# A hybrid RWKV-7 and attention layer: woven products placed at five dense stretches, and five head sums' roots spread to rows through DRAM

## The chip, the cores and the metric

The kernel runs on one core of a Trainium2 chip. The metric is the device time of one execution in microseconds, lower is better. A core has TensorE (PE), VectorE (DVE), ScalarE (ACT), GpSimd (POOL) and SyncE (SP), each with an instruction queue of its own. They meet through semaphores; DMAs are issued from a queue and run beside the engines.

## The reference

One layer computes, for 512 latent tokens on a grid and 128 context tokens of width 1024, an RWKV-7 branch (8 heads of 64, forward and backward), a neighbourhood attention branch, merges and a feed-forward block. Two formulas matter here: the norm of the keys of each head, and the norm of the recurrence's output of each head.

```python
kk = _heads(k * k_k)
kk = kk * lax.rsqrt(jnp.sum(kk * kk, axis=-1, keepdims=True) + L2_EPS)
...
def _wkv_step(s, inp):
    r, w, k, v, a, b = inp
    sa = jnp.einsum("bhvk,bhk->bhv", s, a)
    s = s * w[:, :, None, :] + sa[..., None] * b[:, :, None, :] + v[..., None] * k[:, :, None, :]
    return s, jnp.einsum("bhvk,bhk->bhv", s, r)
...
y = y_f + y_b
mean = jnp.mean(y, axis=-1, keepdims=True)
var = jnp.mean(jnp.square(y - mean), axis=-1, keepdims=True)
y = (y - mean) * lax.rsqrt(var + GN_EPS) * _heads(ln_g) + _heads(ln_b)
out = (y + bonus).reshape(bsz, t_len, RW_WIDTH) * gate
```

## The kernel before

After modulation, norm, the input products and the attention (0 to about 250 us) comes the recurrence (about 250 to 640 us), then the merges and the feed-forward block. Tiles hold channels on the 128 partitions and the 640 tokens along the row; a tile of 128 channels is two heads. The recurrence therefore runs over four groups, `ct` = 0 to 3, of two heads each. The tokens are cut into ten blocks of 64, for two directions: 20 lines.

A group has three parts, each a Python generator:

- `main` (two steps): `n_job` (L1191), small products that make the triangular matrices `Nt`.
- `inv`: inverts them. VectorE makes a chain of 30 steps `s` = 1 to 30 on the tile `RL` (L1297, then the pairs L1328 and L1332, or L1321), and transposes the result at L1345 and L1347, which TensorE reads at L1358. Beside the chain, at the steps in `jobs` (2, 9 and 28; in group 3: 2, 8 and 28), stand jobs of TensorE: `v_job` (L1248), `t_job` (64 products of 64x64, L1270) and `g_job` (128 more, L1212, L1215, L1248, L1259). Their masks (L1229, L1232) are VectorE's.
- `carry`: the state's chain over the blocks (TensorE L1399 to L1461, ScalarE L1422 and L1454, VectorE L1473), with `prep` of the next group beside it.

`out(ct - 1)`, the end of the group before (norm of each head, bonus, gate), and `bonus(ct)` (L1159 on TensorE, L1161 on VectorE) are advanced inside `inv(ct)`. `out(3)` comes behind the last carry.

The order on each engine is the order in which the program is written. The generator `weave` sets it: at every `yield` it takes the next entry of `PRM["plan"]`, three numbers: so many woven products, then so many steps of `out`, then of `bonus`. A woven product is a 128x128 by 128x320 product of another stage (L225, L589), of which there is a supply in every group; it depends on nothing in the recurrence. The weights of these products come as a high and a low half; the low half is made by an accumulating DMA from GpSimd's queue (L193).

Two places take a head's sum to all rows. In `prep_a` (L666 to L686) five products sum the squares of the keys into a tile `r` of [128 tokens x 10] (5 token blocks x 2 heads), GpSimd takes the power -1/2 (L671), ScalarE copies each value 64 times along the row (L676), TensorE transposes the five blocks (L681), and VectorE multiplies the keys by the result from PSUM (L684, L686) into `kk`. `out` does the same with `inv_sqrt_bcast` (L1130 sums, L1134, L1136 power, L1139 copy, L1144 transposes), and multiplies at L1497 and L1498. The steps of `out` stand between steps of the inverse's chain in VectorE's order.

Of the kernel before, what the change touches and what calls it, by code (L numbers as in the profile page):

```python
# [14 lines left out]
P = 128  # L15
# [12 lines left out]
    order=("l0 l1 k0 r0 v0 l2 g0 g1 g2 k1 g3 r1 g4 g5 v1 g6 g7 k2 r2 g8 g9 v2 g10 g11 k3 r3 g12 g13 v3 g15 g14 a0 a1 a2 "  # L28
     "a3 b0 b1 b2 b3"),
    plan=(  # L30
        "22.0 0.0 2.0 4.0",
        ("0.0.0 2.0.0 2.0.1 10.0.0 2.0.1 2.0.1 2.0.1 2.0.1 2.0.1 2.0.0 10.0.0 2.0.0 2.0.0 10.0.0 2.0.0 "
         "2.0.0 2.0.0 10.0.0 2.0.0 2.0.0 2.0.0 2.0.0 2.0.0 2.0.0 2.0.0 2.0.0 2.0.0 2.0.0 2.0.0 2.0.0 "
         "5.0.0 24.0.0 20.0.0 10.0.0 8.0.0 8.0.0 0.0.0"),
        ("10.0 1.0 7.1 5.2 0.0 7.1 7.2 0.0 7.1 7.2 0.0 8.1 12.2 0.0 7.1 7.2 0.0 7.1 7.2 0.0 6.1 6.2 "
         "0.0 8.1 7.2 6.0"),
        "22.0 2.0 2.0 2.0",
        ("0.0.0 0.0.0 2.0.1 10.0.0 1.0.0 2.1.1 2.1.1 2.1.1 2.1.1 1.1.1 10.0.0 3.1.0 2.0.0 2.0.0 2.0.0 "
         "2.1.0 2.1.0 10.0.0 2.1.0 2.1.0 2.1.0 2.1.0 2.1.0 2.1.0 12.0.0 2.0.0 2.0.0 2.0.0 2.0.0 2.0.0 "
         "5.0.0 24.0.0 20.0.0 10.0.0 8.0.0 8.0.0 0.0.0"),  # L40
        ("10.0 0.0 7.1 7.2 0.0 7.1 7.2 0.0 7.1 7.2 0.0 7.1 7.2 0.0 7.1 7.2 0.0 6.1 7.2 0.0 7.1 7.2 0.0 "
         "7.1 7.2 6.0"),
        "22.0 2.0 0.0 5.0",
        ("0.0.0 10.0.0 2.0.1 10.0.0 2.0.0 2.1.1 2.1.1 2.1.2 2.1.1 2.1.0 10.0.0 2.0.0 2.0.0 2.0.0 2.1.0 "
         "2.1.0 2.1.0 10.0.0 2.1.0 2.1.0 2.1.0 3.1.0 4.1.0 2.1.0 2.0.0 2.0.0 2.0.0 4.0.0 2.0.0 2.0.0 "
         "5.0.0 24.0.0 18.0.0 8.0.0 9.0.0 8.0.0 0.0.0"),
        ("10.0 0.0 8.1 14.2 0.0 7.1 7.2 0.0 7.1 7.2 0.0 0.1 6.2 0.0 7.1 7.2 0.0 7.1 7.2 0.0 7.1 7.2 "
         "0.0 7.1 7.2 6.0"),
        "32.2 0.0 0.0 0.0",
        ("0.0.0 16.1.0 8.1.1 9.0.0 2.1.0 8.1.1 1.1.1 0.1.1 0.1.1 0.1.1 4.1.0 14.1.0 6.1.0 6.1.0 6.1.0 "  # L50
         "6.1.0 6.1.0 7.1.0 6.0.0 6.0.0 6.0.0 6.0.0 6.0.0 6.0.0 7.0.0 6.0.0 6.0.0 6.0.0 6.0.0 6.0.0 "
         "6.0.0 6.0.0 11.0.0 8.0.0 8.0.0 2.0.0 0.0.0"),
        ("10.3 0.0 5.1 5.2 0.0 5.1 5.2 0.0 5.1 5.2 0.0 5.1 5.2 0.0 5.1 5.2 0.0 5.1 5.2 0.0 5.1 5.2 0.0 "
# [63 lines left out]
def body(ctx: ExitStack, tc: tile.TileContext, xs, xp, cols, consts, w_ada, b_row, w_rw, w_qkv,  # L117
# [380 lines left out]
    def pre_t():  # L498
        return kp.tile([P, 643], F32, tag="pre", bufs=4, name=nm("pre"))[:, :NT]
# [131 lines left out]
    def parts(ct, k):  # L631

        return ((0, 320), (320, NT)) if ct and PRM[k] else ((0, NT),)

    def prep_a(ct, S, tpps, mid=None):

        S.Dt = kp.tile([P, 2, 10], F32, tag="Dt", bufs=2, name=nm("Dt"))
        S.P65 = [None, None]
        S.pre = []
        S.BK = []  # L640

        def lora(d, tw, ta):
# [25 lines left out]
        yield 0, 0  # L668
        rk = kp.tile([P, 10], F32, tag="r10", bufs=2, name=nm("r10"))
        dve.tensor_scalar(out=rk, in0=ps[:, :10], scalar1=1.0, scalar2=1e-12, op0=ALU.mult, op1=ALU.add)  # L670
        pool.tensor_tensor(out=rk, in0=rk, in1=mhalf[:, :10], op=ALU.pow)  # L671
        S.pre.append((pre_t(), pre_t()))
        yield 0, 0.2
        yield from lora(0, *S.pre[0])
        for (a, b) in parts(ct, "pa"):
            act.copy(V(sqt, [[64, (b - a) // 64], [1, 64]], a), V(rk[:, :], [[1, (b - a) // 64], [0, 64]], a // 64))  # L676
        yield 2, 0
        pa, pb = tpps(), tpps()
        for i in range(5):
            o_ = pa[:, i * 128:(i + 1) * 128] if i < 4 else pb[:, :128]  # L680
            pe.transpose(o_, sqt[:, i * 128:(i + 1) * 128], ident)  # L681
        yield 0, 0
        S.kk = kk = kk_t()
        dve.scalar_tensor_tensor(out=kk[:, :512], in0=kt_[:, :512], scalar=col("kk", ct),  # L684
                                 in1=pa[:, :512], op0=ALU.mult, op1=ALU.mult)
        dve.scalar_tensor_tensor(out=kk[:, 512:], in0=kt_[:, 512:], scalar=col("kk", ct),  # L686
                                 in1=pb[:, :128], op0=ALU.mult, op1=ALU.mult)
        yield 0, 1.2
# [24 lines left out]

# [385 lines left out]
    with ExitStack() as s3:  # L1099
# [23 lines left out]
        def wps():  # L1123
            return pp.tile([P, 512], F32, tag="w", bufs=6, name=nm("w"))

        def inv_sqrt_bcast(sqt, scale, eps, ps_):

            ps = ps_()
            for i in range(5):
                pe.matmul(ps[:, 2 * i:2 * i + 2], sqt[:, i * 128:(i + 1) * 128], kc("blk2", 2),  # L1130
                          start=True, stop=True)
            yield
            r = kp.tile([P, 10], F32, tag="r10", bufs=2, name=nm("r10"))
            dve.tensor_scalar(out=r, in0=ps[:, :10], scalar1=scale, scalar2=eps, op0=ALU.mult,  # L1134
                              op1=ALU.add)
            pool.tensor_tensor(out=r, in0=r, in1=mhalf[:, :10], op=ALU.pow)  # L1136
            yield
            yield
            act.copy(c64(sqt), V(r[:, :], [[1, 10], [0, 64]]))  # L1139
            yield  # L1140
            pa, pb = ps_(), ps_()
            for i in range(5):
                o = pa[:, i * 128:(i + 1) * 128] if i < 4 else pb[:, :128]
                pe.transpose(o, sqt[:, i * 128:(i + 1) * 128], ident)  # L1144
            yield
            return pa, pb
# [146 lines left out]
        def inv(ct, S, late):  # L1293
# [11 lines left out]
            for s in range(1, 31):  # L1305
# [178 lines left out]
        def out(ct, S):  # L1484
# [4 lines left out]
            for hf in range(2):  # L1489
# [7 lines left out]
            dve.tensor_tensor(out=yc[:, :512], in0=yc[:, :512], in1=pa[:, :512], op=ALU.mult)  # L1497
            dve.tensor_tensor(out=yc[:, 512:], in0=yc[:, 512:], in1=pb[:, :128], op=ALU.mult)  # L1498
# [901 lines left out]
```

## Time and profile before

| | before |
|---|---|
| median of the runs (lowest to highest), us | 1136.23 (1135.29 to 1136.40) |
| the profiled execution, us | 1135.23 |
| its span, us | 1133.1 |
| mean granted TensorE clock | 0.997 |
| TensorE busy in the span | 97% |
| VectorE, ScalarE, GpSimd busy | 72%, 50%, 22% |

The span runs from the first to the last instruction in the trace; 2.1 us of the execution lie around it. A row of a timeline gives start and length in us, engine, line, operation, output and input tiles, shape and count; a bracket at its end is the idle time of the engine ahead of it and what ended it. "issue" there means that the trace shows nothing that the engine waited for.

### The profile page before, as it was taken

To read this page: it belongs to the slowest core of one execution; us is meant where nothing else is said; L and a number is where in the kernel's file an instruction comes from. 1 tells how busy PE (TensorE), PEld (TensorE's weight loads), DVE (VectorE), ACT (ScalarE), POOL (GpSimd) and SP (SyncE) were. 2 spreads that over 40 slices of the span, in tenths; PEclk is the share of its full clock that TensorE was granted. 3 is DMA by queue.
4 is the path that set the end of the run, shared out by engine and by line. 5 is a ranking of instruction groups with operands and counts; after the bars stand their busy time and mean duration, and the time that the engine had idled before them with its cause. 6 is when DMAs were issued, how large, how long until landed. Compare 5 with 4: busy or idle time off the path is not lost. (4 is left out here: it accounts for less than half of the span.)

```text
span 1133.1 us, 27124 instructions
## 1 busy us (share of the span) xinstructions
PE 1098.5 (97%) x11118; PEld 971.1 (86%) x11118; DVE 814.1 (72%) x1709; ACT 571.8 (50%) x1106; POOL 245.7 (22%) x318
## 2 busy tenths in 40 slices
PE   6999999999999999999899999999999999999998
PEld 4688878789888988888898788998999989989987
DVE  4565465669648937946787846899788887889854
ACT  4444566665566575467443534564453543444430
POOL 1163234321101111210100431151212122131100
PEclk9999999999999999999999999999999999999999
DMA  9753677644423453353743873477567567665622
GB/s 340 270 105 103 186 263 264 209 140 120 123 60 93 109 140 88 95 134 78 262 129 107 256 226 121 139 179 185 139 176 181 145 157 178 173 169 143 157 85 93
DMA packets 72995, 179.05 MB, mean 158 GB/s; under 512 B 8708, under 2 KB 23684, under 8 KB 72872
## 3 DMA queue, kind: packets, MB, share of 16 engines
q1 hardware_dynamic: 58488, 140.86, 37.8%
q0 software_dynamic: 12368, 33.56, 16.2%
q10 hardware_dynamic: 2016, 2.90, 0.8%
q8 instruction: 87, 1.43, 0.5%
q14 instruction: 36, 0.29, 0.1%
HBM read 137.81 MB, written 16.94 MB: 137 GB/s over the span
## 5 line engine op out<-in xcount | busy, mean ns | idle before, releaser
L1929 PE MATMUL f<-t,whi 128*128 128x320 f32 x640 | 141.8, 309 | 0.8 <-ACT whi L1974 0.5
L1929 PE MATMUL f<-b,whi 128*128 128x320 f32 x608 | 135.1, 310 | 0.4 <-DVE b L214 0.4
L225 PE MATMUL fl<-h,whi 128*128 128x320 f32 x672 | 121.1, 320 | 0.1
L1929 PEld LDWEIGHTS f<-t,whi 128*128 128x128 f32 x640 | 106.8, 188 | 1.4 <-ACT whi L1974 0.7
L225 PEld LDWEIGHTS fl<-h,whi 128*128 128x128 f32 x672 | 101.4, 188 | 4.9 <-issue 0.2
L1929 PEld LDWEIGHTS f<-b,whi 128*128 128x128 f32 x608 | 101.8, 188 | 1.2 <-issue 0.6
L1929 PE MATMUL f<-t,wlo 128*128 128x320 f32 x320 | 99.0, 309 | 0.2 <-DVE wlo L1977 0.2
L1929 PE MATMUL f<-b,wlo 128*128 128x320 f32 x304 | 94.0, 309 | 0.1
L194 ACT CAST whi<-wst 128x1024 fp32r<-128x1024 f32 (+1 forms) x67 | 69.0, 1031 | 38.6 <-PE acc L313 27.3
L313 PE MATMUL acc<-whi,h 128*128 128x512 f32 x240 | 78.5, 401 | 0.6 <-DVE h L438 0.6
L1974 ACT CAST whi<-ws 128x1024 fp32r<-128x1024 f32 x40 | 42.1, 1052 | 68.9 <-PE f L1929 42.2
L193 POOL DMA_DIRECT2D wlo<-wst x28 | 24.9, 888 | 192.6 <-ACT wlo L192 176.4
L197 DVE TENSOR_TENSOR wlo<-wst,whi 128x1024 fp32r<-128x1024 f32 (+2 forms) x47 | 48.1, 1033 | 25.7 <-ACT whi L194 25.5
L225 PE MATMUL fl<-h,wlo 128*128 128x320 f32 x336 | 62.7, 317 | 0.0
L1929 PEld LDWEIGHTS f<-t,wlo 128*128 128x128 f32 x320 | 60.1, 188 | 0.5 <-DVE wlo L1977 0.5
L1473 DVE TENSOR_TENSOR ZV<-w,Dt 64x128 f32<-64x128 f32 x64 | 18.4, 288 | 54.5 <-PE w L1461 53.3
L1929 PEld LDWEIGHTS f<-b,wlo 128*128 128x128 f32 x304 | 57.1, 188 | 0.4 <-DVE wlo L1977 0.4
L1988 POOL TENSOR_TENSOR ws<-wst 128x512 f32<-128x512 f32 x20 | 30.8, 1542 | 121.0 <-DVE wlo L1977 81.5
L1977 DVE TENSOR_TENSOR wlo<-ws,whi 128x1024 fp32r<-128x1024 f32 x40 | 53.7, 1342 | 4.1 <-ACT whi L1974 4.1
L313 PEld LDWEIGHTS acc<-whi,h 128*128 128x128 f32 x240 | 44.8, 188 | 12.5 <-issue 2.2
L225 PEld LDWEIGHTS fl<-h,wlo 128*128 128x128 f32 x336 | 51.2, 188 | 1.9
L984 POOL TENSOR_TENSOR L<-L,m 128x384 f32<-128x384 f32 (+1 forms) x40 | 32.1, 824 | 94.0 <-DVE m L983 75.1
(379 smaller groups left out, 2826.4 us busy)
## 6 DMA issues: line engine op xcount, KB each, us to landing
wst<-in_w_dram SPq DMA_DIRECT2D x58, 512.0 KB
wst<-in_w_rw_dram SPq DMA_DIRECT2D x31, 512.0 KB
wlo<-wst POOLq DMA_DIRECT2D x28, 512.0 KB, 4.8
wa<-in_w_ada_dram SPq DMA_DIRECT2D x24, 512.0 KB
f<-in_w_ada_dram SPq DMA_DIRECT2D x16, 512.0 KB
t<-in_w_dram SPq DMA_DIRECT2D x16, 512.0 KB
wst<-in_w_qkv_dram SPq DMA_DIRECT2D x12, 512.0 KB
o<-o_d SPq DMA_DIRECT2D x14, 320.0 KB
```

The lines of the kernel that those rows point to most:

```text
L193: pool.dma_start(lo[:, :n].bitcast(F32), st[:, :n], accum_op=ALU.add)
L194: act.copy(hi[:, :n], st[:, :n])
L197: dve.tensor_tensor(out=lo[:, a:b], in0=st[:, a:b], in1=hi[:, a:b].bitcast(F32), op=ALU.subtract)
L225: pe.matmul(ps[:, :t1 - t0], w[:, a:a + 128], x[:, k0 + kt, t0:t1], start=n == 0, stop=n == 3 * nk - 1)
L313: pe.matmul(pss[i][:, a:b], lhs(x, kt, ts_), w[:, cs_], start=ki == 0 and n == 0, stop=ki == last and n == 2)
L984: pool.tensor_tensor(out=L, in0=L, in1=V(m[:, :], [[0, w]], 3), op=ALU.mult)
L1473: dve.tensor_tensor(out=V(ZV[own, l + 1, h, :], [[128 * dl, 2], [1, 64]]), in0=V(pn[own, :], [[64, 2], [1, 64]], 64 * g), in1=V(Dt[own, 0, ...
L1929: pe.matmul(ps[:, :H2], w_[:, c_], x_[:, kt, :], start=first and kt + n == 0, stop=last and kt == 3 and n == 2, skip_group_check=more)
L1974: act.copy(r[0][:, :width], src())
L1977: dve.tensor_tensor(out=r[1][:, :width], in0=src(), in1=r[0][:, :width].bitcast(F32), op=ALU.subtract)
L1988: eng_x(PRM["se"][i - 1]).tensor_tensor(out=o_, in0=x, in1=y, op=op)
```

## The change

It has two parts.

The numbers of `plan` move woven products; within each group their sum stays. In group 0, six go from behind the first job of `inv` (step 2) to between the two jobs of `main`. In group 1, six go from behind that job to the start of `inv`, ahead of it. In groups 2 and 3 a new tuple `cut` names steps at which `inv` yields between `t_job` and `g_job`, so that an entry of the plan falls there: ten products at step 9 of group 2; two at step 28 of group 2, with six more ahead of `t_job`; six at step 8 of group 3, with three and four more at the two entries ahead. These came later in their groups before.

A new function `spread` takes the place of the copy, the transposes and the read from PSUM, in `prep` of groups 1, 2 and 3 (`if ct`) and in `out` of groups 0 and 1 (`far`). It writes `r` turned to DRAM, [10 x 128], and reads it back, each value to 64 rows, with one DMA for each head. All three DMAs stand on GpSimd's queue. VectorE then multiplies once, from SBUF. In `prep` the product moves behind the first direction's `exp` of `tw`; in `out` the number of yields stays.

```diff
     plan=(
-        "22.0 0.0 2.0 4.0",
-        ("0.0.0 2.0.0 2.0.1 10.0.0 2.0.1 2.0.1 2.0.1 2.0.1 2.0.1 2.0.0 10.0.0 2.0.0 2.0.0 10.0.0 2.0.0 "
+        "22.0 6.0 2.0 4.0",
+        ("0.0.0 2.0.0 2.0.1 4.0.0 2.0.1 2.0.1 2.0.1 2.0.1 2.0.1 2.0.0 10.0.0 2.0.0 2.0.0 10.0.0 2.0.0 "
...
-    wl="dddddddddppppppppppppppppppppppdddpdddd", nu=9, lg=14, jo=(2, 0, 1), na=(
+    wl="dddddddddppppppppppppppppppppppdddpdddd", nu=9, lg=14, jo=(2, 0, 1), cut=((), (), (9, 28), (8,)), na=(
...
+    def spread(r, t):
+
+        r_d = dp.tile([10, P], F32, name=nm("r_d"))
+        pool.dma_start(r_d.rearrange("c p -> p c"), r)
+        for h in range(2):
+            x = r_d[h]
+            pool.dma_start(V(t[hrows[h], :], [[128, 5], [1, 128]]),
+                           bass.AP(x.tensor, x.offset, [[0, 64], [256, 5], [1, 128]]))
...
         pool.tensor_tensor(out=rk, in0=rk, in1=mhalf[:, :10], op=ALU.pow)
+        if ct:
+            spread(rk, sqt)
...
+            if ct and not d:
+                dve.scalar_tensor_tensor(out=kk, in0=kt_, scalar=col("kk", ct), in1=sqt, op0=ALU.mult, op1=ALU.mult)
+                yield 0, 0.8
...
             pool.tensor_tensor(out=r, in0=r, in1=mhalf[:, :10], op=ALU.pow)
+            if far:
+                spread(r, sqt)
+                for _ in range(4):
+                    yield
+                return None, None
...
                     for f in (v_job, t_job):
                         f(S, *jobs[s])
+                    if s in PRM["cut"][ct]:
+                        yield
                     masks.append(g_job(S, *jobs[s]))
...
-            pa, pb = yield from inv_sqrt_bcast(ysq, 1.0 / 64, 64e-5, wps)
-            dve.tensor_tensor(out=yc[:, :512], in0=yc[:, :512], in1=pa[:, :512], op=ALU.mult)
-            dve.tensor_tensor(out=yc[:, 512:], in0=yc[:, 512:], in1=pb[:, :128], op=ALU.mult)
+            pa, pb = yield from inv_sqrt_bcast(ysq, 1.0 / 64, 64e-5, wps, ct < 2)
+            if ct < 2:
+                dve.tensor_tensor(out=yc, in0=yc, in1=ysq, op=ALU.mult)
+            else:
...
```

How it moves instructions. First TensorE in `inv` of group 2, at step 9, where `t_job` ends and `g_job` begins. Before:

```order
L1270 MATMUL w_6206<-K,f_833_5751 64x64
L1270 MATMUL w_6207<-K,f_833_5751 64x64
L1248 MATMUL w_6242<-K,vp_627 64x64 x2
L1212 MATMUL w_6243<-AG,f_833_5751 64x64 x2
L1215 MATMUL w_6244<-R__2901,f_833_5751 64x64
```

And now, with L1290 for L1270, L1268 for L1248 and L1232 for L1212; `fl` is the output of the woven products:

```order
L1290 MATMUL w_6194<-K,f_830_5734 64x64
L225 MATMUL fl_6122<-h_95,whi_5855 128x320
L225 MATMUL fl_6122<-h_92,whi_5855 128x320
L225 MATMUL fl_6122<-h_96,whi_5855 128x320
L225 MATMUL fl_6122<-h_92,whi_5855 128x320
L225 MATMUL fl_6122<-h_96,whi_5855 128x320
L225 MATMUL fl_6122<-h_89,wlo_5856 128x320 x2
L225 MATMUL fl_6122<-h_90,wlo_5856 128x320 x2
L225 MATMUL fl_6122<-h_91,wlo_5856 128x320
L1268 MATMUL w_6239<-K,vp_627 64x64 x2
L1232 MATMUL w_6240<-AG,f_830_5734 64x64 x2
```

Ten woven products that stood behind the whole job now stand between its two halves.

Second GpSimd's queue in `inv` of group 1, behind the power for `out(0)`. `U` is a tile of ScalarE's, `wlo` the low half of the next weights. Before:

```order
L1136 TENSOR_TENSOR r_725_4666<-r_725_4666,mhalf 128x10
L538 MEMSET U_4794 128x2
L539 MEMSET U_4794 128x1
L193 DMA wlo_4825<-wst_4602 128x1024
L214 TENSOR_TENSOR out_4627<-out_4627,yo_4898 128x320 x2
```

And now:

```order
L1151 TENSOR_TENSOR r_724_4660<-r_724_4660,mhalf 128x10
L638 DMA r_d_4663<-r_724_4660 128x10x1
L641 DMA pre_4622<-r_d_4663 64x5x128 x2
L538 MEMSET U_4792 128x2
L539 MEMSET U_4792 128x1
L193 DMA wlo_4822<-wst_4532 128x1024
L214 TENSOR_TENSOR out_4621<-out_4621,yo_4887 128x320 x2
```

Three DMAs stand ahead of the memsets and the next weight's DMA; the reads (L641) wait for the write's landing.

Third TensorE in the carry of group 0, where `prep(1)` transposed. Before:

```order
L225 MATMUL fl_3951<-h_92,whi_3719 128x320
L225 MATMUL fl_3951<-h_96,whi_3719 128x320
L681 MATMUL w_3986<-K,pre_3856 128x128 x4
L681 MATMUL w_3987<-K,pre_3856 128x128
L1419 MATMUL w_3998<-ZV,AG 64x64 x4
L1399 MATMUL w_3807<-TG,ZV 64x64 x4
```

And now (L1441 for L1419, L1421 for L1399):

```order
L225 MATMUL fl_3955<-h_92,whi_3719 128x320
L225 MATMUL fl_3955<-h_96,whi_3719 128x320
L1441 MATMUL w_3991<-ZV,AG 64x64 x4
L1421 MATMUL w_3807<-TG,ZV 64x64 x4
L1421 MATMUL w_3808<-TG,ZV 64x64 x4
```

The five transposes are gone, and the carry's products follow the same woven products directly.

More of the change, by code (lines that the diff above doesn't have):

```diff
@@ L37 @@
         "22.0 2.0 2.0 2.0",
-        ("0.0.0 0.0.0 2.0.1 10.0.0 1.0.0 2.1.1 2.1.1 2.1.1 2.1.1 1.1.1 10.0.0 3.1.0 2.0.0 2.0.0 2.0.0 "
+        ("6.0.0 0.0.0 2.0.1 4.0.0 1.0.0 2.1.1 2.1.1 2.1.1 2.1.1 1.1.1 10.0.0 3.1.0 2.0.0 2.0.0 2.0.0 "
          "2.1.0 2.1.0 10.0.0 2.1.0 2.1.0 2.1.0 2.1.0 2.1.0 2.1.0 12.0.0 2.0.0 2.0.0 2.0.0 2.0.0 2.0.0 "
@@ L43 @@
         "22.0 2.0 0.0 5.0",
-        ("0.0.0 10.0.0 2.0.1 10.0.0 2.0.0 2.1.1 2.1.1 2.1.2 2.1.1 2.1.0 10.0.0 2.0.0 2.0.0 2.0.0 2.1.0 "
-         "2.1.0 2.1.0 10.0.0 2.1.0 2.1.0 2.1.0 3.1.0 4.1.0 2.1.0 2.0.0 2.0.0 2.0.0 4.0.0 2.0.0 2.0.0 "
-         "5.0.0 24.0.0 18.0.0 8.0.0 9.0.0 8.0.0 0.0.0"),
+        ("0.0.0 10.0.0 2.0.1 10.0.0 2.0.0 2.1.1 2.1.1 2.1.2 2.1.1 2.1.0 10.0.0 0.0.0 2.0.0 2.0.0 2.0.0 2.1.0 "
+         "2.1.0 2.1.0 10.0.0 2.1.0 2.1.0 2.1.0 3.1.0 4.1.0 2.1.0 2.0.0 2.0.0 2.0.0 4.0.0 8.0.0 2.0.0 2.0.0 "
+         "5.0.0 16.0.0 18.0.0 8.0.0 9.0.0 8.0.0 0.0.0"),
         ("10.0 0.0 8.1 14.2 0.0 7.1 7.2 0.0 7.1 7.2 0.0 0.1 6.2 0.0 7.1 7.2 0.0 7.1 7.2 0.0 7.1 7.2 "
@@ L49 @@
         "32.2 0.0 0.0 0.0",
-        ("0.0.0 16.1.0 8.1.1 9.0.0 2.1.0 8.1.1 1.1.1 0.1.1 0.1.1 0.1.1 4.1.0 14.1.0 6.1.0 6.1.0 6.1.0 "
+        ("0.0.0 16.1.0 8.1.1 9.0.0 2.1.0 8.1.1 1.1.1 3.1.1 4.1.1 6.0.0 0.1.1 1.1.0 4.1.0 6.1.0 6.1.0 6.1.0 "
          "6.1.0 6.1.0 7.1.0 6.0.0 6.0.0 6.0.0 6.0.0 6.0.0 6.0.0 7.0.0 6.0.0 6.0.0 6.0.0 6.0.0 6.0.0 "
@@ L674, in prep_a @@
         yield from lora(0, *S.pre[0])
[L675 to L682, printed above, removed]
-        S.kk = kk = kk_t()
[L684 to L688, printed above, removed]
+        S.kk = kk = kk_t()
+        if ct:
+            yield 2, 0
+        else:
+            act.copy(c64(sqt), V(rk[:, :], [[1, 10], [0, 64]]))
+            yield 2, 0
+            pa, pb = tpps(), tpps()
+            for i in range(5):
+                o_ = pa[:, i * 128:(i + 1) * 128] if i < 4 else pb[:, :128]
+                pe.transpose(o_, sqt[:, i * 128:(i + 1) * 128], ident)
+            yield 0, 0
+            for (a, b, p_) in ((0, 512, pa), (512, NT, pb)):
+                dve.scalar_tensor_tensor(out=kk[:, a:b], in0=kt_[:, a:b], scalar=col("kk", ct),
+                                         in1=p_[:, :b - a], op0=ALU.mult, op1=ALU.mult)
+            yield 0, 1.2
         for d in range(2):
@@ L1124, in wps, with inv_sqrt_bcast @@
             return pp.tile([P, 512], F32, tag="w", bufs=6, name=nm("w"))
-        def inv_sqrt_bcast(sqt, scale, eps, ps_):
+        def inv_sqrt_bcast(sqt, scale, eps, ps_, far):
             ps = ps_()
@@ L1495, in out @@
                 yield
-            pa, pb = yield from inv_sqrt_bcast(ysq, 1.0 / 64, 64e-5, wps)
-            dve.tensor_tensor(out=yc[:, :512], in0=yc[:, :512], in1=pa[:, :512], op=ALU.mult)
-            dve.tensor_tensor(out=yc[:, 512:], in0=yc[:, 512:], in1=pb[:, :128], op=ALU.mult)
+            pa, pb = yield from inv_sqrt_bcast(ysq, 1.0 / 64, 64e-5, wps, ct < 2)
+            if ct < 2:
+                dve.tensor_tensor(out=yc, in0=yc, in1=ysq, op=ALU.mult)
+            else:
+                dve.tensor_tensor(out=yc[:, :512], in0=yc[:, :512], in1=pa[:, :512], op=ALU.mult)
+                dve.tensor_tensor(out=yc[:, 512:], in0=yc[:, 512:], in1=pb[:, :128], op=ALU.mult)
             act.activation(yc, yc, AF.Identity, scale=col("lg", ct), bias=col("lb", ct))
```

## The prediction

> **What bounds the kernel now.** I read the page's busy shares first, then the waits of TensorE in the recurrence (250 to 640 us), then the timelines of the places that the change touches. The first fence is the page's busy us, share and instructions of each engine; the second the waits: engine, its instruction, what it waited for, us in total, times, longest.
>
> ```profile
> PE 1098.5 (97%) x11118; PEld 971.1 (86%) x11118; DVE 814.1 (72%) x1709; ACT 571.8 (50%) x1106; POOL 245.7 (22%) x318
> ```
>
> ```profile
> PE w L1212 <- issue: 2.5, 2, 1.4
> PE w L1448 <- ACT x L1422: 2.1, 6, 0.6
> ...
> PE w L1215 <- DVE bv L1161: 1.6, 1, 1.6
> PE w L1215 <- issue: 1.2, 1, 1.2
> PE w L1191 <- issue: 1.0, 1, 1.0
> ...
> PE w L1270 <- issue: 0.9, 1, 0.9
> PE w L1358 <- DVE f L1345: 0.8, 2, 0.4
> ```
>
> TensorE is busy 97% of the span, so time comes out only where TensorE issues less or waits less. Five of these rows hold six single waits of 0.9 to 1.6 us in runs of small products (L1191, L1270, L1212, L1215). "issue" means that nothing in the program released it; I take it for TensorE running ahead of the loading of its own instructions, since these waits lie inside the runs of 64 to 192 small products that a job writes. That cause is inferred. The last row says that VectorE is a second bound: TensorE has twice waited for the inverse's chain on VectorE (L1345, read by L1358).
>
> The end of that chain in groups 1, 2 and 3 (VectorE), and TensorE's first read of it:
>
> ```profile
> 383.83 2.06 DVE L1345 STREAM_TRANSPOSE f<-RL 128x1024 f32<-128x1024 f32 x1
> ...
> 386.04 0.66 PE L1358 MATMUL w<-f,Nt 32*32 32x32 f32 x29 [0.36 <-DVE f L1345]
> ...
> 477.65 2.07 DVE L1345 STREAM_TRANSPOSE f<-RL 128x1024 f32<-128x1024 f32 x1
> ...
> 480.71 0.51 PE L1358 MATMUL w<-f,Nt 32*32 32x32 f32 x18
> ...
> 579.08 2.05 DVE L1345 STREAM_TRANSPOSE f<-RL 128x1024 f32<-128x1024 f32 x1
> ...
> 584.53 0.69 PE L1358 MATMUL w<-f,Nt 32*32 32x32 f32 x29
> ```
>
> In group 1 TensorE starts 0.15 us after the chain (383.83 + 2.06 = 385.89): VectorE sets the end. In group 2 the chain ends at 479.72, and 0.15 later TensorE could start, but it starts at 480.71: VectorE has 0.84 us to spare. In group 3 it has 584.53 - 581.13 - 0.15 = 3.25. So what TensorE saves inside the inverse counts in full in group 3, up to about 0.9 us in group 2, and not at all in group 1 (nor in group 0, the other of the two waits), unless the chain itself gets shorter.
>
> **The change part by part.** *Five transposes less, in five places.* What such a visit costs, from TensorE's timeline in group 1 (start, length of the row, line, count):
>
> ```profile
> 365.90 0.90 PE L225 MATMUL fl<-h,whi 128*128 128x320 f32 x5
> 366.63 0.71 PE L1144 MATMUL w<-K,pre 128*128 128x128 f32 x5
> 367.10 0.83 PE L225 MATMUL fl<-h,whi 128*128 128x320 f32 x4
> 367.76 1.33 PE L225 MATMUL fl<-h,wlo 128*128 128x320 f32 x8
> 368.93 0.75 PE L225 MATMUL fl<-h,whi 128*128 128x320 f32 x4
> ```
>
> Five woven products leave in 0.73 us and eight in 1.17, 0.147 each. From the five transposes to the fifth product behind them pass 1.13 us, of which four products are 0.59: a visit costs 0.54 us. Three lie in the preparations inside the carries of groups 0, 1 and 2, where TensorE goes straight on:
>
> ```profile
> 311.87 1.29 PE L225 MATMUL fl<-h,whi 128*128 128x320 f32 x7
> 313.00 0.71 PE L681 MATMUL w<-K,pre 128*128 128x128 f32 x5
> 313.63 0.45 PE L1419 MATMUL w<-ZV,AG 128*64 128x64 f32 x8
> ```
>
> Three times 0.54 is 1.6 us. The carry is a chain through ScalarE and VectorE too (the 2.1 us at L1448 above), so a part can turn into waiting: I take -1.4, ends -0.8 and -1.6. The later kk product is covered: the first reader of kk is L725 at 328.03, behind 2.13 us in which VectorE is idle, against a pow that ends near 307.5.
>
> ```profile
> 305.56 1.98 POOL L671 TENSOR_TENSOR r<-r,mhalf 128x10 f32<-128x10 f32 x1 [1.92 <-DVE r L670]
> ...
> 327.39 0.61 DVE L1473 TENSOR_TENSOR ZV<-w,Dt 64x128 f32<-64x128 f32 x2 [2.13 <-PE w L1461]
> 328.03 0.83 DVE L725 SCALAR_TENSOR_TENSOR NK<-pre,kk 128x640 f32<-128x640 f32 x1
> ```
>
> The other two visits are in out of groups 0 and 1, inside the inverses of groups 1 and 2, where by the above they are worth nothing by themselves (group 1) or at most what VectorE allows (group 2).
>
> *The trip through DRAM.* In out, VectorE's product (L1497) keeps its place in VectorE's order and now waits for the last of three DMAs that GpSimd issues behind the pow. VectorE is in order: behind the product stand the next steps of the inverse's chain, so each us that the trip is late is a us of the chain. The time that it has:
>
> ```profile
> 359.52 0.17 DVE L1134 TENSOR_SCALAR r<-w 128x10 f32<-128x10 f32 x1 [0.22 <-PE w L1130]
> 360.17 0.49 DVE L1161 TENSOR_TENSOR bv<-w,vp 128x320 f32<-128x320 f32 x1 [0.48 <-PE w L1159]
> ...
> 369.07 0.68 DVE L1497 TENSOR_TENSOR out<-out,w 128x512 f32<-128x512 f32 x1
> 369.67 0.28 DVE L1498 TENSOR_TENSOR out<-out,w 128x128 f32<-128x128 f32 x1
> ...
> 359.77 1.98 POOL L1136 TENSOR_TENSOR r<-r,mhalf 128x10 f32<-128x10 f32 x1 [5.99 <-DVE r L1134]
> ...
> 454.39 2.08 POOL L1136 TENSOR_TENSOR r<-r,mhalf 128x10 f32<-128x10 f32 x1 [7.58 <-DVE r L1134]
> ...
> 462.89 0.67 DVE L1497 TENSOR_TENSOR out<-out,w 128x512 f32<-128x512 f32 x1
> ```
>
> Group 1: 369.07 - 361.75 = 7.3 us, or 6.8 if the 0.48 us wait goes (below). Group 2: 462.89 - 456.47 = 6.4 us.
>
> The trip L is not in the trace. Its parts have neighbours: GpSimd's DMAs of 128 rows, and one of 256 pieces (128x2x512).
>
> ```profile
> 866.57 1.22 POOL L2077 DMA_DIRECT2D t<-in_w_dram  x1
> ...
> L193 POOL DMA_DIRECT2D wlo<-wst x28 | 24.9, 888 | 192.6 <-ACT wlo L192 176.4
> ...
> wlo<-wst POOLq DMA_DIRECT2D x28, 512.0 KB, 4.8
> ...
> q0 software_dynamic: 12368, 33.56, 16.2%
> ```
>
> A 512 KB load lands 4.8 us after its issue; its data take 0.524 of 33.56 MB of 16.2% of 1133 us, 2.9 us, so a hop without data is 1.9. The 128 further pieces cost 1.22 - 0.88 us, 2.7 ns each. The write has 1280 pieces of four bytes, each read 320. With nothing for further pieces, two hops and the second read's issue (0.5) are 4.3 us. With 2.7 ns each for 1152 and 192 further pieces, 3.1 and 0.5 more, 0.9 for a second read of that size, and up to 1.9 us for 80 tiny packets on each of 16 queues (an estimate at 24 ns), 10.2. Part of the issuing and moving should overlap; I take L = 7.6, ends 4.3 and 10.2. The Trainium skill speaks against this part: "DMA: Bandwidth & Descriptors", Rules for kernel authors, has a strided last dimension become one descriptor per element, which is what the count of 1280 assumes. The same page, Anatomy of one DMA — SWDGE (gpsimd) path, puts a fixed 2.0 us on a DMA (the 1.9 above agrees) and calls descriptor generation small; by that L would be near 4.5 and the total below -5.0 us, while the 0.88 against 1.22 us above says that pieces do cost.
>
> *Group 1.* Six woven products move ahead of the first job (L1248, L1270), whose 0.9 us wait they should mostly fill; six fewer follow. TensorE then reaches the sums (L1130) and the bonus (L1159) about 0.9 earlier, and VectorE's waits of 0.22 and 0.48 for them go: -0.70. One VectorE product over 640 columns (0.83 at L725) for the pair at L1497 and L1498 (369.07 to 369.95) saves some 0.07. The chain ends at L - 6.8 - 0.77 from today's, never better than -0.77: 0.0 at 7.6, ends -0.8 and +2.6.
>
> *Group 2.* The cut puts ten products between t_job and g_job (the 1.2 us wait at L1215), and eight more stand around the second job (1.4 at L1212). With the transposes TensorE saves up to 2 us, VectorE grants 0.84 + 0.07; late by L - 6.4, the group comes to L - 7.3: +0.3, ends -0.9 and +2.9.
>
> *Group 3.* No trip here; the transposes stay. Thirteen products move ahead of g_job, seven before t_job and six behind it, 1.9 us of work:
>
> ```profile
> 554.35 0.28 PE L1215 MATMUL w<-R__2901,f 64*64 64x64 f32 x3 [1.64 <-DVE bv L1161]
> 557.13 0.21 PE L1212 MATMUL w<-AG,f 64*64 64x64 f32 x1 [1.40 <-issue]
> ```
>
> They cover the 1.64 us wait for bv, which does not hang on them. Of the 1.40 I count 0.3, since a run of over a hundred small products remains behind. VectorE's 3.25 us of slack lets it through: -1.9, ends -1.2 and -2.8.
>
> *Group 0.* Six products split a run in main (the 1.0 us wait at L1191), six fewer follow. TensorE waits for VectorE at the end of that inverse, so the chain could start no later and end no earlier: 0, ends -0.3 and +0.2.
>
> *GpSimd's queue.* While the reads wait for the write, the next weight load stands behind them:
>
> ```profile
> 367.43 0.92 POOL L193 DMA_DIRECT2D wlo<-wst  x1 [5.59 <-ACT wlo L192]
> ...
> 379.20 1.34 PE L225 MATMUL fl<-h,wlo 128*128 128x320 f32 x8
> ```
>
> It goes at about pow + 6.5, 368.3, one us late; its first user on TensorE is at 379.20 and it lands in 4.8, so it stays hidden: 0.
>
> Sum: -1.4 + 0.0 + 0.3 - 1.9 + 0 = -3.0 us. The profiled execution took 1135.23 us, 1.0 below the median of the runs (1136.23) and inside their spread; I put the difference on the median: 1133.2.
>
> **The rivals.** What a measurement of this kernel can tell from no change is about 0.2%, 2.3 us.
>
> *The trip is late (other side).* At one place, L1497 in groups 1 and 2, both groups lose one for one: the total is 2L - 18.2. It is zero at L = 9.1; at 10.2 it is +2.2 us, and at 10.5 it is 1139.0. For it: 1280 pieces at 2.7 ns, two hops in a row, a dense VectorE. Against it: the 4.3 us floor. Chance 0.32, half of it at or above 10.2, since that end is a sum of four parts of which none is measured here.
>
> *The trip is early.* At 4.3, and up to 6.4, both groups gain what VectorE allows: -1.4 - 0.8 - 0.9 - 1.9 = -5.0, 1131.2. It needs further pieces to cost almost nothing, which is what the skill's page on DMA says of generation; the 0.34 us for 128 more speaks against. Chance 0.20.
>
> *The woven products fill nothing.* If the loading of instructions goes by their count and not by time, the waits only move to the next run of small products: group 3 keeps the bv wait's 1.2, the carries eat the transposes (-0.8), groups 1 and 2 end at +0.7 and +0.3: -1.0, 1135.2. For it: "issue" has no releaser in the trace. Against it: none of these waits lies among woven products. Chance 0.16.
>
> **How the numbers follow.** The forecast (L from 6.4 to 8.0, fills work) has the rest, 0.32, and its own range is 1131.2 to 1134.0. Faster by over 0.2%: 0.32 + 0.20 less 0.04 for the edge, 0.48. Within 0.2%: the third rival and just under half of the first, 0.30. Slower: 0.22, the rest of the first, the edge and trips later than my end (512 KB loads on the same queue) and a weight load that is late after all. The range leaves out the ends: 1131.0 to 1138.6.
>
> **What would show it.** Right: 25 fewer transposes and products of that kind on TensorE; the waits at L1191, L1270, L1212 and L1215 shrink from 7.2 us together to under 4; VectorE waits for a DMA before the product in out by less than 1.2 us; the inverse's end in group 1 is where it was within 0.8 us of its start. Wrong: VectorE idles 2 us or more there and TensorE waits as long at L1358; or a new "issue" wait appears behind the moved products; or VectorE waits in a preparation for kk; or TensorE waits for a lo half of a weight.

## Result: 5% slower, and the profile after

| | before | changed |
|---|---|---|
| median of six runs (lowest to highest), us | 1135.93 (1135.04 to 1138.09) | 1191.61 (1187.86 to 1196.36) |
| the profiled execution, us | 1135.23 | 1192.48 |
| span, us | 1133.1 | 1190.5 |
| mean granted TensorE clock | 0.997 | 0.971 |

The ratio is 1.0495, 95% interval 1.0474 to 1.0516: 55.7 us more where 3.0 less were forecast. First the busy times of the changed kernel (us, share of the span, instructions):

```profile
PE 1113.3 (94%) x11093; PEld 982.0 (82%) x11093; DVE 811.9 (68%) x1704; ACT 567.9 (48%) x1098; POOL 258.8 (22%) x333
```

TensorE runs 25 instructions fewer and is busy 14.8 us longer: the same products take longer, at a lower clock. Where the time lies is seen in a table by stage: length of the stretch, then busy time (and instructions) of TensorE, its weight loads, VectorE, ScalarE, GpSimd, then TensorE's clock and the DMA share. The stretches are carry 0, inverse 1, carry 1, inverse 2, carry 2, inverse 3, and the end of the recurrence with the merges. Before:

```profile
288.60:347.20 58.60, 55.37 (x822) 48.54 (x823) 33.11 (x60) 36.77 (x89) 7.66 (x11) 0.97 0.37 98
347.20:386.00 38.80, 37.40 (x812) 34.74 (x811) 34.95 (x135) 21.35 (x42) 8.54 (x18) 1.00 0.35 95
386.00:438.80 52.80, 51.64 (x814) 45.91 (x814) 32.66 (x59) 35.13 (x86) 10.17 (x14) 1.00 0.43 109
438.80:480.70 41.90, 38.88 (x817) 35.66 (x816) 35.84 (x135) 21.80 (x41) 8.25 (x16) 1.00 0.37 100
480.70:538.20 57.50, 56.41 (x841) 50.00 (x840) 32.33 (x62) 37.22 (x92) 7.78 (x13) 1.00 0.43 108
538.20:584.50 46.30, 43.26 (x859) 41.13 (x858) 37.79 (x137) 23.03 (x46) 6.08 (x10) 1.00 0.64 212
643.90:709.10 65.20, 65.20 (x312) 51.97 (x311) 40.92 (x74) 28.00 (x51) 20.79 (x22) 1.00 0.59 180
```

And the changed kernel:

```profile
288.40:355.70 67.30, 57.73 (x817) 50.41 (x820) 32.91 (x59) 36.24 (x87) 10.12 (x14) 0.92 0.37 89
355.70:402.80 47.10, 39.59 (x807) 36.31 (x807) 34.91 (x134) 20.59 (x41) 11.05 (x21) 0.93 0.34 85
402.80:464.70 61.90, 54.16 (x809) 48.03 (x809) 32.33 (x58) 34.49 (x84) 12.73 (x17) 0.92 0.41 98
464.70:517.10 52.40, 40.64 (x813) 36.82 (x812) 35.21 (x134) 21.06 (x40) 10.71 (x19) 0.87 0.31 85
517.10:585.30 68.20, 57.63 (x836) 50.90 (x835) 34.58 (x61) 36.55 (x90) 10.74 (x16) 0.92 0.39 93
585.30:633.90 48.60, 45.47 (x863) 42.48 (x862) 37.34 (x135) 23.07 (x46) 6.13 (x10) 0.96 0.62 206
693.30:765.60 72.30, 67.65 (x311) 53.92 (x311) 38.15 (x74) 27.65 (x51) 20.26 (x22) 0.95 0.60 191
```

Each of the five places with a trip through DRAM lost 8 to 11 us (8.7, 8.3, 9.1, 10.5, 10.7: 47.3). Inverse 3, which has moved products but no trip, lost 2.3, and the merges, which the change doesn't touch, 7.1.

The trip itself. GpSimd's timeline for out(0) in group 1, then VectorE's product and ScalarE behind it (L1151 is the power, L638 the write, L641 the reads, L1520 the product, L1524 out's affine copy, L542 the copy of a finished unit of woven products):

```profile
367.96 1.99 POOL L1151 TENSOR_TENSOR r<-r,mhalf 128x10 f32<-128x10 f32 x1 [5.68 <-DVE r L1149]
370.25 1.05 POOL L638 DMA_DIRECT2D r_d<-r  x1 [0.30 <-POOL r L1151]
381.33 1.39 POOL L641 DMA_DIRECT2D pre<-r_d  x2 [10.03 <-PE fl L225]
382.71 0.12 POOL L538 MEMSET U<- 128x2 f32 x1
...
385.89 0.83 DVE L1520 TENSOR_TENSOR out<-out,pre 128x640 f32<-128x640 f32 x1 [8.63 <-DMA pre<-r_d]
...
386.75 0.92 ACT L1524 ACTIVATE out<-out,C 128x640 f32<-128x640 f32 x1 [11.20 <-DVE out L1520]
387.58 0.41 ACT L542 COPY U<-fl 128x320 f32<-128x320 f32 x1
```

From the power's end (369.95) to the product pass 15.9 us; this is the trip's length, L in the prediction. The write holds GpSimd 1.05 us, yet the first read goes 11.1 us after the write's start. The releaser in the bracket at L641 is inferred and wrong: the order has the reads wait for the write's landing. A landing is told by sixteen increments of a semaphore; in the trace those of this write arrive between 377.4 and 380.7, though its data packets lie between 372 and 373. VectorE then waits 8.63 us, ScalarE 11.20 us for VectorE, and the woven products for ScalarE's copy. TensorE's longest waits, 240 to 720 us, are these:

```profile
PE fl L225 <- ACT U L542: 18.0, 2, 11.2
PE w L1441 <- DVE ZV L1495: 16.3, 4, 9.0
PE w L1483 <- issue: 4.5, 1, 4.5
```

And what VectorE waited for at the product of the keys (L724, us and times), and at that of out (L1520):

```profile
  DMA pre<-r_d: 25.2, 3
```

```profile
  DMA pre<-r_d: 17.9, 2
```

43.1 us of waiting on VectorE, at five places. In the preparations the carry's own step, L1495, stands behind the product in VectorE's order, and TensorE waits for it. In the carry of group 2:

```profile
555.70 0.89 DVE L724 SCALAR_TENSOR_TENSOR kk<-kt__626,C,pre 128x640 f32<-128x640 f32 x1 [12.54 <-DMA pre<-r_d]
556.61 0.61 DVE L1495 TENSOR_TENSOR ZV<-w,Dt 64x128 f32<-64x128 f32 x2
...
556.95 0.91 PE L1441 MATMUL w<-ZV,AG 128*64 128x64 f32 x7 [8.96 <-DVE ZV L1495]
```

### The profile page after: what moved, and what is told of

Same layout as the page of the kernel before. It is cut to its first block, busy times and chain, and to the rows that moved or that the text cites. A ratio compares the mean times of both kernels' runs of the same rounds, so it can differ in the third digit from the quotient of the medians.

```text
span 1190.5 us, 27089 instructions
## 1 busy us (share of the span) xinstructions
PE 1113.3 (94%) x11093; PEld 982.0 (82%) x11093; DVE 811.9 (68%) x1704; ACT 567.9 (48%) x1098; POOL 258.8 (22%) x333
## 4 chain that ended last, share of the span: by engine, by line
PE 34%; issue 6%; DVE 5%; DMA 5%; ACT 2%; POOL 1%; SPq 0%; DVEq 0%; ACTq 0%; POOLq 0%
PE f L1954 20%; PE acc L313 6%; PE y L2215 4%; PE fl L225 2%; DMA wlo<-wst 1%; DMA wlo<-t 1%; DVE wlo L2002 1%; DMA t<-in_w_dram 1%; DMA wst<-in_w_dram 1%; DMA o<-o_d 0%; ACT wlo L192 0%; DVE hq L1842 0%; DMA wst<-in_w_out_dram 0%; DVE wlo L2128 0%; ACT b L213 0%
## 5 line engine op out<-in xcount | busy, mean ns | idle before, releaser
L225 PE MATMUL fl<-h,whi 128*128 128x320 f32 x672 | 126.3, 329 | 18.0 <-ACT U L542 18.0
L225 PEld LDWEIGHTS fl<-h,whi 128*128 128x128 f32 x672 | 104.7, 194 | 23.8 <-ACT U L542 18.6
L313 PE MATMUL acc<-whi,h 128*128 128x512 f32 x240 | 79.3, 404 | 0.4 <-DVE h L438 0.4
L1495 DVE TENSOR_TENSOR ZV<-w,Dt 64x128 f32<-64x128 f32 x64 | 18.5, 289 | 65.0 <-PE w L1483 53.0
L313 PEld LDWEIGHTS acc<-whi,h 128*128 128x128 f32 x240 | 45.3, 191 | 12.8 <-issue 2.4
```

What stands on the lines that cost most here:

```text
L225: pe.matmul(ps[:, :t1 - t0], w[:, a:a + 128], x[:, k0 + kt, t0:t1], start=n == 0, stop=n == 3 * nk - 1)
L313: pe.matmul(pss[i][:, a:b], lhs(x, kt, ts_), w[:, cs_], start=ki == 0 and n == 0, stop=ki == last and n == 2)
L1495: dve.tensor_tensor(out=V(ZV[own, l + 1, h, :], [[128 * dl, 2], [1, 64]]), in0=V(pn[own, :], [[64, 2], [1, 64]], 64 * g), in1=V(Dt[own, 0, ...
```

## The experiments

Theory 1: the trip alone did it; the write's confirmation is late, whatever stands in order behind it pays, and TensorE's clock is lower on top. Theory 2: the moved woven products share the blame. Theory 3: GpSimd's held queue, or a weight load that is handed on late, is the main thing. Medians stand beside the kernel before on the same chip.

**The moves without the trip.**

```diff
-        if ct:
+        if ct and False:
             spread(rk, sqt)
...
-            pa, pb = yield from inv_sqrt_bcast(ysq, 1.0 / 64, 64e-5, wps, ct < 2)
+            pa, pb = yield from inv_sqrt_bcast(ysq, 1.0 / 64, 64e-5, wps, False)
```

> The changed plan and cut, with the copies, transposes and PSUM products of before in all five places; no trip through DRAM. Theory 1 (the trip alone made the change slow; the moves do what was forecast): about 1133.5 us, 1132.5 to 1135, the waits at L1215 and L1212 of groups 2 and 3 mostly gone, no half-clock stretch beyond those of before. Theory 2 (the moved woven products share the blame: the changed kernel's group 3 took 2.3 us longer and its merges 7.1): 1140 to 1146 us.

1134.48 against 1133.95 us: ratio 1.0001 (0.9989 to 1.0013). Theory 2 in its plain form falls, and so does theory 1's gain of 2 us. All "issue" waits of the recurrence are gone from this kernel's list, 5.6 us, but this stands in it (L597 is ScalarE's Tanh that empties a bank of the gate unit, L1525 out's affine copy), with ScalarE's rows:

```profile
PE fl L225 <- ACT fl L597: 2.5, 1, 2.5
PE w L1236 <- DVE bv L1182: 0.4, 1, 0.4
```

```profile
549.49 0.92 ACT L1525 ACTIVATE out<-out,C 128x640 f32<-128x640 f32 x1 [3.42 <-DVE out L1524]
550.31 0.74 ACT L597 ACTIVATE fl<-fl 128x320 f32<-128x320 f32 x2
```

In group 3 the thirteen products that moved forward are the first of a new unit. Its PSUM banks are empty only after L597, which stands on ScalarE behind a copy that waits 3.42 us for VectorE. Of the 3.0 us that TensorE waited for bv and at L1212 before, 2.5 came back there (the 0.4 us for bv lies in another group); inverse 3 took 46.16 us against 46.32.

**The trip without the moves.**

```diff
-cut=((), (), (9, 28), (8,))
+cut=((), (), (), ())
```

with the `plan` of before.

> The trip through DRAM in all five places with the plan of before and no cut. Theory 1: about 1191 to 1196 us, as the changed kernel or a little above it, since what the plan gains in groups 1 and 2 is lost behind VectorE anyway. Theory 2: 1180 to 1186 us, 6 to 10 below the changed kernel.

1182.68 against 1133.95 us: 1.043 (1.0412 to 1.0448), 48.7 us more. That is 7 us less than the changed kernel's 55.7, as theory 2 has it, though the moves alone cost nothing. What the two have together is found below, in SyncE's order.

**The trip in the preparations alone, and in out alone.**

> The changed plan and cut, the trip in the three preparations alone; out is as before. In the changed kernel the carries of groups 0, 1 and 2 took 67.3, 61.9 and 68.2 us against 58.6, 52.8 and 57.5. Theory 1 with each place paying for itself: +28.5 us there, 1133.5 + 28.5 = 1162 us, plus 7 if the merges' wait stays. Theory 3 (one late weight load that is handed on from group to group, so that the places multiply each other): under 1155 us.

> The changed plan and cut, the trip in out of groups 0 and 1 alone; the preparations are as before. In the changed kernel the inverses of groups 1 and 2 took 47.1 and 52.4 us against 38.8 and 41.9. Theory 1 with each place paying for itself: 8.3 + 10.5 more, and what the moves save in group 3 off: 1151 to 1154 us, VectorE idle 8 to 9 us ahead of each of the two products. Theory 3: under 1146 us.

1163.09 (1.0256, 1.0231 to 1.0281) and 1156.15 us (1.0194, 1.0178 to 1.0210): 29.1 and 22.2 us more. The first is as theory 1 had it; the second lies 2 us above its range: inverses 1 and 2 took 9.0 and 9.5 us longer than with the moves alone, inverse 3, which has no trip, 3.1 (49.3 us). The sum of the two, 51.3, is near the 48.7 of all five: each place pays for itself, and theory 3's handing on falls.

**The queue alone.** Copies and transposes stay; write and two small reads are issued besides:

```diff
+    def scr():
+        return kp.tile([P, 16], F32, tag="scr", bufs=1, name=nm("scr"))
...
         if ct:
-            spread(rk, sqt)
+            spread(rk, scr())
```

> The kernel with the moves alone, copies and transposes kept, and in the five places the DRAM write of the roots and two small reads (64 pieces of 64 bytes, into a scratch tile that nothing reads) issued besides on GpSimd's queue. No engine but GpSimd waits for the trip. Theory 1 (an engine that stands in order behind the trip pays, here only GpSimd's queue): the memsets of U come 13 to 15 us later, ScalarE's copy of a finished unit and the woven products behind it wait in the two places of out: 2 to 10 us more than the moves alone. Theory 3 (GpSimd's held queue is the main cost of the change): 20 us or more. If the queue has room: no difference.

1148.44 against 1135.95 us: 1.0101 (1.0065 to 1.0136), 11 to 12 us above the moves alone. Theory 3 falls; the time is just over theory 1's 2 to 10, but not by its mechanism. It isn't the places of out that pay (0.5 and 0.3 us) but the carries, 5.6, 4.6 and 5.0 us in the profiled execution. Two rows of waits, then the carry of group 0 on TensorE, ScalarE and GpSimd ("remote" means that the profile names no instruction as releaser):

```profile
PE w L1488 <- ACT ZV L1481: 6.3, 3, 3.1
...
ACT U L542 <- POOL U L539: 4.5, 3, 3.2
```

```profile
314.23 0.40 PE L1475 MATMUL w<-x,Rt 64*64 64x64 f32 x8
314.56 0.56 PE L225 MATMUL fl<-h,whi 128*128 128x320 f32 x2
314.96 0.89 PE L225 MATMUL fl<-h,wlo 128*128 128x320 f32 x5
318.93 0.82 PE L1488 MATMUL w<-ZV,TG 128*64 128x64 f32 x8 [3.08 <-ACT ZV L1481]
...
318.62 0.55 ACT L1481 COPY ZV<-w 64x128 f32<-64x128 f32 x2 [4.01 <-remote]
...
319.18 1.07 POOL L644 DMA_DIRECT2D scr<-r_d  x2 [10.84 <-DMA r_d<-r]
...
320.28 0.12 POOL L538 MEMSET U<- 128x2 f32 x1
```

The memsets of U do come late, and ScalarE waits 4.5 us for them, but those three waits stand in the inverses (at 377.8, 386.2 and 486.9 us). In the carry ScalarE's copy L1481 waits for TensorE's L1475, whose row ends at 314.63. TensorE goes on to seven woven products, but the trace has the increment of its semaphore only at 318.59, and ScalarE starts 0.03 us later. The reads and the memsets behind them, from 319.18 on, come too late to have held it; the four-byte write, issued at 307.29, is what is under way. In the carry of group 1 the same increment comes 3.7 us behind the product; in that of group 2 the 5.0 us are spread over smaller waits.

This isn't of this kernel alone. In each of the six kernels with the four-byte write in the preparations, the trace has increments of TensorE's semaphore there 2 us or more behind the last product that sends one; the other eight, with a packed write there or none, have none over 0.7 us in the recurrence. (Some records of products can be missing, so a single delay is less sure than the pattern.) In the changed kernel it is 5.4 us in the carry of group 0, 318.30 against 312.87, and the 4.5 us "issue" wait at L1483 is TensorE waiting for the ScalarE copy that this held. So the write costs the carries time even where no engine but GpSimd waits for it. Why signals come late beside it isn't shown.

**The pieces.** The write packed, the turning left out:

```diff
-        r_d = dp.tile([10, P], F32, name=nm("r_d"))
-        pool.dma_start(r_d.rearrange("c p -> p c"), r)
+        r_d = dp.tile([P, 10], F32, name=nm("r_d"))
+        pool.dma_start(r_d, r)
```

> The changed kernel, with the roots written to DRAM as they lie, 128 pieces of 40 bytes and not 1280 of 4; the reads are the same in shape, so the turning of the roots is left out and the rows get other values. Theory 1a (the scattered four-byte pieces make the write's last increment arrive 11 to 13 us after its issue): the write is done 3 to 5 us after its issue, the trip takes 8 to 10 us, VectorE waits 1 to 3 us in the two products of out and hardly in the preparations: 1136 to 1144 us. Theory 1b (any write to DRAM takes this long to be confirmed here): 1180 to 1192 us.

1146.70 us, 1.0101 (1.0079 to 1.0123). The same places of its timeline:

```profile
359.74 1.99 POOL L1151 TENSOR_TENSOR r<-r,mhalf 128x10 f32<-128x10 f32 x1 [5.67 <-DVE r L1149]
362.03 0.64 POOL L638 DMA_DIRECT2D r_d<-r  x1 [0.30 <-POOL r L1151]
364.56 1.39 POOL L641 DMA_DIRECT2D pre<-r_d  x2 [1.90 <-ACT ZV L1273]
...
369.38 0.83 DVE L1520 TENSOR_TENSOR out<-out,pre 128x640 f32<-128x640 f32 x1 [0.35 <-DMA pre<-r_d]
```

From write to read 2.5 us, not 11.1; the trip takes 7.65 us and VectorE waits 0.35. Theory 1a holds: it is the 1280 scattered four-byte pieces. Their number, their size and their scatter in DRAM changed together here and aren't told apart. In the preparations VectorE still waited 6.1 us for the reads, where hardly any was expected, but the three carries took only 0.4 us more in all than with the moves alone. The time lies 2.7 us above its range, for a reason that SyncE's order, below, shows.

**Another queue.** `pool.dma_start` becomes `sp.dma_start` in `spread`.

> The changed kernel with all three DMAs of a trip on SyncE's queue instead of GpSimd's. Theory 1a (the pieces, whoever issues them): the write is as slow, 1180 to 1195 us, more if weight loads behind it on SyncE's queue come late. Rival (GpSimd's software queue makes the write slow): the trip falls under 8 us and the time under 1145 us.

1184.50 us, 1.0437 (1.0409 to 1.0465); the first read goes 9.5 to 11.5 us after the write. It is not GpSimd's path. On this queue the trace shows the pieces one by one: in the first out, 1296 packets of four bytes (the 1280 pieces and 16 more) all start within 0.8 us, from 366.8 to 367.6, and the sixteen increments arrive from 373.7 to 375.3. The pieces pass quickly; the confirmation is late.

**The Tanh copies early.**

```diff
-            later(lambda hf=hf, a=a, b=b: rest(hf, a, b))
+            rest(hf, a, b)
```

> The kernel with the moves alone, and the two Tanh copies that empty the gate unit's two PSUM banks (L597) written at the end of the unit, ahead of out's affine copy on ScalarE, not three entries of the plan later. With the moves alone TensorE waited 2.54 us for them in group 3, at the first woven product of the next unit, and the moves changed the time by nothing. Theory 1 (that wait ate the gain of group 3): 2 to 2.6 us less than the moves alone, 0.2% faster than the kernel before. Rival (VectorE's chain is the bound in group 3 too once TensorE is ahead, or the next wait stands right behind): the same as the moves alone within 1 us.

1139.24 against 1135.95 us: 1.0042 (1.0027 to 1.0057). Slower; both theories missed. The 2.54 us wait is gone and inverse 3 is 0.25 us shorter: with TensorE earlier at the same small products, a wait without a releaser of 1.1 us is back. But the part after the recurrence got 4.7 us longer, with a 3.7 us wait for a low half at L313, of the kind that the changed kernel has there:

```profile
PE acc L313 <- DMA wlo<-wst: 4.7, 1, 4.7
```

SyncE's timeline tells the kernels apart: before, and the changed kernel:

```profile
633.52 1.85 SPq L1708 DMA_DIRECT2D tr<-trw_d  x4
635.42 10.90 SPq L176 DMA_DIRECT2D wst<-in_w_out_dram  x3
```

```profile
692.54 0.33 SPq L176 DMA_DIRECT2D wst<-in_w_out_dram  x1
692.93 2.84 SPq L1733 DMA_DIRECT2D tr<-trw_d  x4
695.82 1.06 SPq L176 DMA_DIRECT2D wst<-in_w_out_dram  x2
```

One weight load of the later merge has come ahead of the four loads of tr and of two weights that are needed first. SyncE's order, unlike that of the other engines here, isn't the order of the program: a scheduler sets it when the kernel is built. The changed kernel, the packed write, SyncE's trip and the early Tanh copies have the load ahead, and take 554 to 557 us from the last inverse to the end; the others so far have it behind, and take 548.5 to 549.6.

**The load put back**, in the changed kernel, with the packed write, and with the early Tanh copies:

```diff
+            if o_w.get(src.offset) == 6:
+                with tc.issue_after(seen[0].ins):
+                    sp.dma_start(st[:, :n], src)
```

> The changed kernel with nothing altered but one weight load on SyncE's queue: in the changed kernel a load of the merge's output weight (in_w_out) stands ahead of the four loads of tr, in the kernel before behind them and two more weight loads; here it is put back there. In the traces the four kernels with the load ahead took 554 to 557 us from the last inverse's end to the end of the program, those with it behind 549 to 550, with a wait of TensorE for a low half (L313) of 3.7 to 4.7 us. Theory (the flip is a cost of its own): 5 to 8 us less than the changed kernel, 1183 to 1187 us. Rival (the late wait comes from the trips, the flip is chance): 1190 us or more.

> The kernel with the packed write (128 pieces of 40 bytes, the turning of the roots left out) with the same load of SyncE's queue put back. Theory: 5 to 7 us less than the packed write alone (1.0101 of the kernel before), 1.004 to 1.006 of it; what is left is the trip's remaining lateness in out and group 3. Rival: unchanged at 1.010.

> The moves alone with the early Tanh copies, and the load of SyncE's queue put back. With the load ahead it was 1.0042 of the kernel before, its tail 4.7 us longer than that of the moves alone. Theory: 0.998 to 1.000 of the kernel before, its group 3 0.2 to 0.4 us shorter than with the moves alone. Rival (the tail is its own): 1.003 or more.

1182.16 (1.0405, 1.0378 to 1.0432), 1139.86 (1.0032, 1.0014 to 1.0051) and 1134.55 us (0.9999, 0.9984 to 1.0014) against 1136.10. The changed kernel loses 10 us by the medians, 7 by its last part (549.75 us, not 556.65); the packed write 7 to 8, the early copies 5. The flip is a cost of its own, a little over the sizes that were expected. It also settles the trip without the moves: with the order put back the changed kernel is 46.1 us above the kernel before, and that one, which had the old order, 48.7, with intervals that overlap. The early copies didn't gain what was expected of them: inverse 3 took 46.19 us, as with the moves alone, since 1.2 us of "issue" and 0.8 us for a DMA took the place of the 2.5.

**The moves of groups 0 to 2 alone**, with SyncE's order of before:

> The moves of groups 0 to 2 without those of group 3 (no trip, copies and transposes kept), SyncE's queue in the order of before. Group 3 then keeps the wait of 1.6 us for bv and that of 1.4 us at L1212, and does not have the 2.5 us wait for the Tanh copies. Theory 1 (the moves of group 3 only trade one wait for another): within 0.5 us of the moves alone, 0.998 to 1.000 of the kernel before. Rival (group 3's moves were worth 2 us, and other places lost it): 2 us slower than the moves alone.

1135.11 us: 0.9991 (0.9978 to 1.0004). No gain that can be told from none, and none lost by leaving group 3 out. Its own inverse 3 took 49.1 us. The two waits for bv and at L1212 stand there again, now L1245 and L1242:

```profile
551.70 0.28 PE L1245 MATMUL w<-R__2901,f 64*64 64x64 f32 x3 [1.64 <-DVE bv L1191]
554.75 0.26 PE L1242 MATMUL w<-AG,f 64*64 64x64 f32 x1 [1.66 <-issue]
```

From 553.6, within the second of them, TensorE ran 6.8 us at half clock; the kernel before passed its two (1.64 and 1.40) at full clock.

## Why the prediction was wrong

*The trip's length* is the step that failed. L was put at 7.6 us, ends 4.3 and 10.2; it was 15.9 and 16.1 in out and 17 to 18 in the preparations. Of its parts the fixed hop (1.9) was near: the packed write took 2.5 in out, and its trip 7.65. Pieces were priced by what they cost GpSimd to issue, 2.7 ns each, and there they cost next to nothing: 1280 pieces held it 1.05 us, against 0.64 for 128. The other price in the upper end, 24 ns a packet on a queue, stands in no row; from SyncE's queue all the pieces passed in 0.8 us. What the pieces did cost was in no row of the trace before: the time until DRAM confirms them, 8 us and more. The rival's form, 2L - 18.2, was right in out: 15.9 and 16.1 against budgets of 7.3 and 6.4 give 8.6 and 9.7, and VectorE waited 8.63 and 9.24. Its size was outside the end that I had built. For the two groups alone it gives 2 x 15.9 - 14.9 = 16.9 us, where inverses 1 and 2 lost 18.5 with the trip in out alone, and inverse 3 another 3.1. Three of the signs named for a wrong forecast came: VectorE idle over 2 us ahead of the product in out, VectorE waiting for kk in the preparations, and TensorE waiting for a low half.

Weighed again, the Trainium skill's rule against a strided last dimension ("DMA: Bandwidth & Descriptors", Rules for kernel authors), by which it becomes one descriptor per element, spoke rightly: SyncE's queue shows the 1280 packets. The same page's fixed 2.0 us (Anatomy of one DMA — SWDGE (gpsimd) path), which it lays mostly to the confirmation in the target memory, agrees with the packed write (2.5 us) and not with 1280 pieces (10.5 and 10.8 us until the sixteenth increment, in the two places where the trace has all sixteen). By the prediction's own bounds its L near 4.5 would have given -5.0 us, not less.

*The preparations' cover* failed with it. The cover was read from the first user of kk, L725, some 20 us behind the power. But VectorE is in order there as well: behind the waiting product stood the carry's step L1473 (now L1495), for which TensorE waited 16.3 us. In the kernel with the packed write VectorE came to the product 4.8 to 9.4 us behind the power; that is the true cover. I had asked this of out and not of the preparations. -1.4 became +29. About half of that isn't this order at all: in the kernel of the queue alone, where VectorE waits for no trip, the three carries lost 15 us, in the first two with TensorE's signals 3.7 and 4.0 us late.

*GpSimd's queue* was costed by the weight load alone. The memsets of U, named in the order of the change, were passed over. They do come late, but no run shows them to cost much: in the kernel of the queue alone the inverses where ScalarE waits for them took 0.5 and 0.3 us longer.

*TensorE's clock* was left out. Busy time rose by 14.8 us with fewer instructions, at 0.87 to 0.93 in the five stretches. The stretches at half clock in the trace are 3.4, 6.8, 10.2 and 13.7 us long, where TensorE has waits of up to 11 us; before the change, one of 3.4 us stood in the recurrence. The Trainium skill ("TensorE: Matmul & The Clock Gate", HAM oscillation — how this bites in real kernels) has an idle window of some 3.4 us halve the clock. The long waits agree with that; the two waits of the last experiment, 1.64 and 1.66 us, are each shorter than that and went with half clock all the same, so it isn't the whole rule here.

*SyncE's queue* had no term, because the change writes nothing to it. Its order flipped all the same: 7 to 10 us.

*The moves*: right that woven products remove the "issue" waits in the kernel with the moves alone; that the cause is the loading of instructions is still inferred. They can come back: with the same moves, a wait of 1.1 to 1.5 us without a releaser stands in inverse 3 of the early Tanh copies, the packed write and the trip in out alone, which is what the third rival said. Wrong that the removed waits are time: group 3's -1.9 was -0.16, since another wait stood right behind. The total of the moves, about none, is near the third rival's, in group 3 by another mechanism.

What adds up: the trip with four-byte pieces, 42.3 us (1182.16 less 1139.86); what is left with the packed write, 3.8; SyncE's order, 6.9 by the last part. That is 53.0 of the 55.7, and the rest is within the intervals. (By the medians SyncE's order is 9.6, but that is a difference with which the sum must close.)

What stays open is what of the pieces, their number, size or scatter, makes the confirmation late; why TensorE's signals come late beside it; why the preparations' writes took 11 to 13.5 us until the read and those in out 11.1 to 11.4; and how much of the 42 us would go at full clock alone.

## What to carry to other kernels

A turn through DRAM is priced by its confirmation and by everything in order behind whoever waits for it, on each engine; and a write in over a thousand tiny pieces can slow engines that don't wait for it at all. Write it in rows, or don't make it. A gap that is filled on the busiest engine is a gain only if the next wait there is later than the gap was long. Look at the queues that the change doesn't write: a scheduler may have moved them.

## What the runs showed of the hardware that I had not expected

A DMA of 5 KB in 1280 four-byte pieces to DRAM held its issuer 1.05 us. Its sixteenth increment came 10.5 and 10.8 us after its start in the two places of out; in the preparations, where the trace lacks some increments, the last one that it has came 10.6 to 12.9 us after. From SyncE's queue it was no faster (9.5 to 11.5 us to the read). The same 5 KB in 128 pieces took 2.4 to 2.5 us to the read in the inverses and 4.0 to 5.3 us in the carries. While such a four-byte write was under way in a carry, increments of TensorE's semaphore came up to 5.4 us behind the product that sends them, and ScalarE stood still for up to 5.5 us. And two waits of TensorE, 1.64 and 1.66 us with 1.4 us of products between them, went with 6.8 us at half clock in one kernel, and two of 1.64 and 1.40 with none in another.
